# Gathers beside the first table: 28 dense expert columns for 48, and one pace for 58 gathered bursts

## The chip, the core and the metric

One NeuronCore of a Trainium2 chip runs the whole program in one launch. The engines are TensorE (PE; PEld is its weight load), VectorE (DVE), ScalarE (ACT), GpSimd (POOL) and SyncE (SP); 16 DMA engines move data between HBM and the on-chip memory SBUF. TensorE's sums lie in PSUM, eight banks of 128 partitions x 512 floats. The metric is the device time of one execution in microseconds (us), the median of several.

## The reference

A decoder layer on 256 tokens of width 2048: an RMSNorm with adaptive shift and scale, a token mixer (recurrent and state-space heads), and then PEER, a mixture of 128 x 128 = 16,384 one-neuron experts. The change lies in PEER alone, which is this:

```python
q = jnp.einsum("bsd,de->bse", h, w_q)...            # 8 heads, two halves of 128
sub_val, sub_idx = lax.top_k(sub, 16)               # 16 best of 128 keys per half
cand_idx = sub_idx[..., 0, :, None] * 128 + sub_idx[..., 1, None, :]
top_val, top_pos = lax.top_k(cand_val, 16)          # 16 of 256 pairs per head
gate = jax.nn.softmax(top_val, axis=-1)
act = jax.nn.gelu(jnp.einsum("td,thkd->thk", xt, u_tab[e]))
out = jnp.einsum("thk,thkd->td", g * act, v_tab[e])  # 128 experts a token
```

So each token has 128 (expert, gate) pairs. The expert number is 128 i + j. The kernel's inputs lay both tables out by the second key j: a "column" is the 128 experts with one j, 1 MB of U and 1 MB of V.

## The kernel before

All products are split into a high and a low part (`issue_split`: ScalarE copies the rounded half, VectorE subtracts), so a weight tile of 128 x 1024 floats ("tick", 0.5 MB) needs one ScalarE and one VectorE instruction. Tiles are loaded four ahead (NRAW) and split four ahead (NHL).

PEER treats columns in two ways. The first J1 = 80 columns (`u_quad`, 20 blocks of four columns, 160 ticks of 12 matmuls, lines 1467 to 1469): the product of every token with every expert goes to a DRAM array `ad`. For their second table, the (token, expert) pairs are sorted into lists: 32 tokens form a block g, 128 list places a row m; four blocks with the same m make a "quad". There are two lists (tokens 0 to 127, 128 to 255) of GL = 23 rows each, 46 quads. A quad's work: four indirect DMAs fetch one number each per place out of `ad` (`w_gather`, line 1519), four fetch 128 rows of V, 8 KB each (`v_gather`, line 1509), into one of seven row buffers; `w_make` applies the gelu and the gate and spreads the result over a 128 x 32 matrix per block; `v_quad` (line 1541) multiplies, 16 matmuls of 32 columns. Sums stay in PSUM banks 0 to 3 until a list is done.

The last JD = 48 columns are dense: `u_slot` (two ticks a column, lines 453 and 455) gives all tokens' products, times a dense table `Wt` of gates; `v_slot` (line 1637, two ticks a column, one for each half of the width) multiplies with V.

The order on every engine is written out by hand. Steps beside the main loop stand in a background queue `bg` that each tick pays for with 1.0 (`bg_pay`), a step costing 1.3 to 3.5; `defer` puts the elementwise half of a step behind the next tick. In `u_quad` these are the top-16 searches, the first list (`l_step`, `l_dec`), and 32 steps of the dense table (`g_step`: VectorE makes one-hot matrices, GpSimd multiplies in two halves of the gate, TensorE sums, ScalarE evacuates). The second list is made in the dense ticks, every fourth of which runs one list step (`tick`). From there a pace spreads the quads: quad q runs once q < 44 (n - 3) / 188 at dense tick n. The seven row buffers are filled before (`rows_first`). `gate2_tick` takes the last section of the adaLN product along on VectorE.

## Time and profile before

| | |
|---|---|
| time, median of 3 | 2092.22 us (2092.17 to 2098.64) |
| profiled execution | 2095.62 us, its span 2093.9 us |
| PE busy | 2017.4 us (96%) |
| DVE, ACT, POOL busy | 71%, 46%, 36% |
| DMA | 620.50 MB, 296 GB/s over the span |
| first table by blocks (`u_quad`) | 847 to 1337 us, DMA at 238 GB/s |
| dense columns, first table (`u_slot`) and quads | 1337 to 1703 us, DMA at 368 GB/s |
| dense columns, second table (`v_slot`) and quads | 1703 to 2065 us, DMA at 381 GB/s |

The page's rows of busy tenths cut the span into 40 slices; the windows view gives the busy time of each engine in chosen stretches; the DMA view gives packets, bytes and the share of the 16 engines' time by queue: q1 is SP's, q10 ScalarE's, q0 GpSimd's indirect DMAs.

### The profile page before, as it was taken

The numbers are of one execution on the slowest core, as the hardware profiler recorded it, in microseconds if no ns is written. First come the engines' busy times: TensorE is split into PE (matmuls) and PEld (weight loads), VectorE is DVE, ScalarE is ACT, GpSimd is POOL, SyncE is SP. The second block draws the span as 40 slices with busy tenths as digits, with TensorE's granted clock in tenths as the row PEclk, the third lists the DMA queues.
The fourth block names the chain that finished last, engine by engine and source line by source line (L and its number), as shares of the span: only waits on it lengthen the run. The fifth ranks groups of instructions, "written<-read, shape, count | busy, mean of one in ns | idle before, by whom it ended". The sixth has DMA issues, their size and how long they took to land. (4 is left out here: it accounts for less than half of the span.)

```text
span 2093.9 us, 34021 instructions
## 1 busy us (share of the span) xinstructions
PE 2017.4 (96%) x12742; PEld 1624.9 (78%) x12742; DVE 1489.5 (71%) x2211; ACT 963.7 (46%) x1457; POOL 745.6 (36%) x600
## 2 busy tenths in 40 slices
PE   7999999999999999999999999999999999998996
PEld 4789998989999898888787777776777766666663
DVE  3368897898878868879979999766555445454444
ACT  3446665677744454444443454433333333333332
POOL 0013344232212010000500477565556545554553
PEclk9999999999999999999999999999999999999999
DMA  9967767778789955668786677789999979999993
GB/s 387 406 233 250 230 225 230 230 241 295 273 295 344 332 177 181 197 224 278 228 272 214 204 258 247 251 336 407 387 400 394 407 280 404 420 411 362 417 412 113
DMA packets 237949, 620.50 MB, mean 296 GB/s; under 512 B 25352, under 2 KB 109496, under 8 KB 215480
## 3 DMA queue, kind: packets, MB, share of 16 engines
q1 hardware_dynamic: 188992, 387.76, 53.4%
q0 software_dynamic: 32384, 175.44, 20.9%
q10 hardware_dynamic: 16400, 55.06, 7.1%
q8 instruction: 102, 1.67, 0.3%
q14 instruction: 71, 0.58, 0.1%
HBM read 621.07 MB, written 14.72 MB: 304 GB/s over the span
## 5 line engine op out<-in xcount | busy, mean ns | idle before, releaser
L148 ACT ACTIVATE hl<-raw 128x1024 fp32r<-128x1024 f32 x594 | 628.8, 1061 | 1001.9 <-PE b L455 214.4
L157 DVE TENSOR_TENSOR hl<-raw,hl 128x1024 fp32r<-128x1024 f32 x594 | 765.0, 1295 | 114.6 <-ACT hl L148 102.5
L453 PE MATMUL b<-H,hl 128*128 128x512 f32 x1376 | 494.0, 402 | 1.4 <-ACT X L674 1.0
L455 PE MATMUL b<-H,hl 128*128 128x256 f32 x1376 | 385.7, 280 | 2.4 <-DVE hl L157 2.4
L453 PEld LDWEIGHTS b<-H,hl 128*128 128x128 f32 x1376 | 259.1, 188 | 81.0 <-issue 19.4
L1637 PE MATMUL b<-hl,X 128*128 128x512 f32 x1152 | 271.5, 394 | 11.5 <-DVEq L1753 6.4
L1637 PEld LDWEIGHTS b<-hl,X 128*128 128x128 f32 x1152 | 215.0, 189 | 77.5 <-issue 25.8
L455 PEld LDWEIGHTS b<-H,hl 128*128 128x128 f32 x1376 | 260.3, 189 | 4.0 <-DVE hl L157 3.1
L1467 PE MATMUL b<-hl,H 128*128 128x512 f32 x640 | 255.0, 398 | 0.0
L1469 PE MATMUL b<-hl,H 128*128 128x512 f32 x640 | 250.4, 391 | 2.2 <-DVE hl L157 2.2
L1468 PE MATMUL b<-hl,H 128*128 128x512 f32 x640 | 249.7, 390 | 0.0
L1519 POOL DMA_INDIRECT X<-ad,X x184 | 205.6, 1117 | 83.0 <-issue 55.7
L1541 PE MATMUL b<-tk,Wz 128*32 128x512 f32 x848 | 169.7, 602 | 7.5 <-DVE X L1531 4.6
L1509 POOL DMA_INDIRECT tk<-in_v_t,X x106 | 126.6, 1195 | 140.4 <-PE b L1541 116.1
L808 PE MATMUL b<-H,hl 128*128 128x256 f32 x560 | 162.9, 291 | 0.4 <-DVE ggt L465 0.4
L810 PE MATMUL b<-H,hl 128*128 128x256 f32 x560 | 159.5, 285 | 1.3 <-DVE hl L157 1.3
L809 PE MATMUL b<-H,hl 128*128 128x256 f32 x560 | 159.5, 285 | 0.0
L1541 PE MATMUL b<-vq,Wz 128*32 128x512 f32 x624 | 144.2, 598 | 0.4 <-DMA vq<-in_v_t,X 0.4
L1469 PEld LDWEIGHTS b<-hl,H 128*128 128x128 f32 x640 | 120.4, 188 | 28.8 <-DVE hl L157 3.0
L1468 PEld LDWEIGHTS b<-hl,H 128*128 128x128 f32 x640 | 120.8, 189 | 23.5
L393 DVE SCALAR_TENSOR_TENSOR adacc<-adr,cact,adacc 128x1024 f32<-128x1024 f32 x90 | 124.7, 1385 | 20.1 <-DMA adr<-in_w_ada 20.0
L1467 PEld LDWEIGHTS b<-hl,H 128*128 128x128 f32 x640 | 120.6, 188 | 23.0
(373 smaller groups left out, 3199.8 us busy)
## 6 DMA issues: line engine op xcount, KB each, us to landing
raw<-in_u_t SPq DMA_DIRECT2D x208, 512.0 KB
raw<-in_w_in SPq DMA_DIRECT2D x146, 512.0 KB
adr<-in_w_ada SPq DMA_DIRECT2D x96, 512.0 KB
adw<-in_w_ada SPq DMA_DIRECT2D x64, 512.0 KB
raw<-in_w_o SPq DMA_DIRECT2D x64, 512.0 KB
raw<-in_u_t ACTq DMA_DIRECT2D x48, 512.0 KB
raw<-in_v_t SPq DMA_DIRECT2D x48, 512.0 KB
raw<-in_v_t ACTq DMA_DIRECT2D x48, 512.0 KB
```

What stands on the lines that cost most here:

```text
L148: act.activation(t[:, 0], r, AF.Copy)
L157: dve.tensor_sub(t[:, 1], r, t[:, 0].bitcast(FT))
L453: pe.matmul(ps, w[:, 0, c], x[:, k].rearrange("p a b -> p (a b)"), start=(k == first), stop=False, skip_group_check=True)
L455: pe.matmul(ps[:, :256], w[:, 1, c], x[:, k, 0], start=False, stop=(k == 15), skip_group_check=True)
L808: pe.matmul(ps, wh, hT[:, k, 0, :], start=(k == 0), stop=False)
L809: pe.matmul(ps, wh, hT[:, k, 1, :], start=False, stop=False)
L1467: pe.matmul(o, hh, w[:, 0, :, kk], start=(k == 0), stop=False)
L1468: pe.matmul(o, hl_, w[:, 0, :, kk], start=False, stop=False)
L1469: pe.matmul(o, hh, w[:, 1, :, kk], start=False, stop=(k == 15))
L1519: pool.indirect_dma_start(wA[:, n % 32:n % 32 + 1], None, adf, bass.IndirectOffsetOnAxis(ap=LW[:, tb, g, m:m + 1], axis=0), bounds_check=T ...
L1541: pe.matmul(sb[c][32 * g:32 * g + 32, :], Wz[:, q % NW, g], vs[(4 * q + g) % NROW][:, c * 512:(c + 1) * 512], start=(m == 0), stop=(m == G ...
L1637: pe.matmul(ob[tb * 2 + c], w[:, i, s], v[:, k, c * 512:(c + 1) * 512], start=(jj == 0 and (i, k) == (0, 0)), stop=(jj == JD - 1 and k == 1))
```

## The change

JD falls to 28, so that 100 columns are gathered and `u_quad` has 25 blocks, 200 ticks. Each list gets two parts: places 0 to 13 (GA) hold experts with j < 48, places 14 to 28 (GB) those with 48 <= j < 100; GL is 29 and there are 58 quads. `ad` becomes two arrays, the first of which is complete after 12 of the 25 blocks. Both lists are now made inside `u_quad`, ahead of the dense table's steps. When the first list is done, `open_sparse` starts gathers, and from then on one counter of ticks, first-table and dense ticks alike, paces all quads. Their order is: list 0 first part, list 1, list 0 second part; the first part's sums are stashed in `S0` and added later. Row buffers: six from then on, eight once the first table is done. PSUM: first-table sums rotate through banks 0 to 2, lists and dense-table steps share bank 3, quads have banks 4 to 7. The dense table's gate multiply is one VectorE operation on both halves. The fallback `spill` follows the split of `ad`; it does not run with these inputs.

GpSimd, around the first gathers. `tk`, `vq`, `vx` are row buffers, `ohr`, `lists` and `two` hold lists and one-hot matrices, X_8024 and `lsm` the gathered numbers and list tables. Before (the dense table's multiplies, then the last rows and the first weight gathers, at the end of `u_quad`):

```order
L1372 TENSOR_TENSOR ohr<-ohr,lists 128x8x48
L1373 TENSOR_TENSOR ohr<-ohr,lists 128x8x48
L1694 MEMSET vq_12931 128x2048
L1509 DMA vq_12931<-in_v_t,X_8024 128x2048
L1694 MEMSET vq_12936 128x2048
L1509 DMA vq_12936<-in_v_t,X_8024 128x2048
L1519 DMA X_8024<-ad,X_8024 128x1 x9
L1509 DMA tk<-in_v_t,X_8024 128x2048
```

Now (at tick 112 of 200):

```order
L1539 MEMSET tk 128x2048 x4
L1539 MEMSET vq_10822 128x2048
L1539 MEMSET vx 128x2048
L1562 DMA lsm<-ad_8715,X_8024 128x1
L1549 DMA tk<-in_v_t,X_8024 128x2048
...
L1549 DMA vx<-in_v_t,X_8024 128x2048
L1562 DMA lsm<-ad_8715,X_8024 128x1 x12
```

The buffers are cleared together before the first gather, weight gathers stand between the row gathers, and the multiplies are gone from the engine.

TensorE, between two first-table ticks (a new place for a quad; before, only list and dense-table steps stood between first-table ticks):

```order
L1501 MATMUL b_12283<-hl,H 128x512
L1590 MATMUL b_11493<-vq_10822,Wz 32x512
L1590 MATMUL b_11493<-vx,Wz 32x512
L1590 MATMUL b_11493<-tk,Wz 32x512 x2
L1590 MATMUL b_11494<-vq_10822,Wz 32x512
...
L1590 MATMUL b_11496<-tk,Wz 32x512 x2
L1499 MATMUL b_12282<-hl,H 128x512
```

The quad's sums (b_11493 to b_11496, one bank each) stay open over such ticks; the next tick's matmuls stand behind the quad.

ScalarE, at the dense table's steps (`Wt`, its evacuation; `hl`, the split of a weight tile). Before, and then now:

```order
L148 ACTIVATE hl<-raw 128x1024
L1450 ACTIVATE Wt<-b_11320 128x8x24 x2
L148 ACTIVATE hl<-raw 128x1024
L1450 ACTIVATE Wt<-b_11363 128x8x24 x2
L148 ACTIVATE hl<-raw 128x1024 x2
```

```order
L149 ACTIVATE hl<-raw 128x1024
L1576 ACTIVATE lsm<-lsm 128x4
L149 ACTIVATE hl<-raw 128x1024
L1483 ACTIVATE Wt<-b_12261 128x8x14 x2
L149 ACTIVATE hl<-raw 128x1024
L1483 ACTIVATE Wt<-b_12308 128x8x14 x2
```

The order of split and evacuation is kept, a quad's gelu (`lsm`) stands between, and b_12261 and b_12308 are now the same bank where b_11320 and b_11363 were two.

The diff, cut to its core:

```diff
-JD = 48
+JD = 28
...
-GL = 23
+JA = 48
+GA, GB = 14, 15
+GL = GA + GB
...
 def p_ew2():
+            dve.tensor_tensor(pos, pa, V[0], op=OP.mult)
+            dve.scalar_tensor_tensor(x, pb, 128.0 * GA, V[1], op0=OP.add, op1=OP.mult)
+            dve.tensor_tensor(pu, pos, x, op=OP.add)
...
         if e == 15:
-            bg.extend(fin_steps())
-            bg.extend(l_step(0, n) for n in range(16))
-            bg.append((None, lambda: l_dec(0), 1.5))
+            f1, f2 = fin_steps()
+            bg.extend(f1)
+            bg.extend(l_step(0, n) for n in range(5))
+            bg.extend(f2)
+            bg.extend(l_step(0, n) for n in range(5, 16))
+            bg.append((None, lambda: (l_dec(0), open_sparse()), 2.0))
+            bg.extend(l_step(1, n) for n in range(16))
+            bg.append((None, lambda: (l_dec(1), sq.update(lists=False)), 2.0))
             bg.extend(g_step(n) for n in range(32))
...
 def prep():
-            dve.tensor_tensor(o[:, :, 1, :], bc(LS["iota16"][:, None, J1:], 128, NG, JD),
+            e = LS["eg"][:, n % 2]
+            dve.tensor_tensor(e, bc(LS["iota16"][:, None, J1:], 128, NG, JD),
                               bc(jT[:, s, None], 128, NG, JD), op=OP.is_equal)
-            pool.tensor_tensor(o[:, :, 0, :], o[:, :, 1, :], bc(LS["fld"][:, 2, s, None], 128, NG, JD), op=OP.mult)
-            pool.tensor_tensor(o[:, :, 1, :], o[:, :, 1, :], bc(LS["fld"][:, 3, s, None], 128, NG, JD), op=OP.mult)
+            dve.tensor_tensor(o, bc(e[:, :, None, :], 128, NG, 2, JD),
+                              bc(LS["fld"][:, 2:4, s].rearrange("p f t -> p t f")[:, :, :, None], 128, NG, 2, JD),
+                              op=OP.mult)
...
 def u_quad(n, pay):
-        ps = [bank(2 * (n % 2) + tb) for tb in range(2)]
+        ps = [bank((2 * n + tb) % 3) for tb in range(2)]
         for kp in range(8):
-            for kk in range(2):
-                k = 2 * kp + kk
-                for tb in range(2):
+            for kk, tb in ((0, 0), (1, 0), (0, 1), (1, 1)):
+                    k = 2 * kp + kk
...
+            if kp == 7:
+                t = keep.tile([128, 2, 512], FT, name="X2")
+                for tb in range(2):
+                    act.activation(t[:, tb], ps[tb], AF.Copy)
...
-            if it >= 22 and it % 2 == 0:
+            if it >= 22 and it % 2 == 0 or it >= 160:
                 gt["slot"] = it
                 gate2_tick()
+            tick()
...
+    quads = ([(0, m) for m in range(GA)] + [(1, m) for m in range(GL)] + [(0, m) for m in range(GA, GL)])
+    def v_feed(k=99):
+        while free and k and sq["g"] < 4 * NQD:
+            q, g = divmod(sq["g"], 4)
+            tb, m = quads[q]
+            if sq["lists"] and tb:
+                return
+            x = buf[sq["g"]] = free.pop(0)
+            pool.indirect_dma_start(x, None, vf, bass.IndirectOffsetOnAxis(ap=LV[:, tb, g, m:m + 1], axis=0),
+                                    bounds_check=E1 - 1, oob_is_err=False)
...
+    def w_feed(k=99):
+        while k and sq["w"] < 4 * min(NQD, sq["n"] + 4):
...
+            i = int(m >= GA)
+            if i and not sq["stored"] or sq["lists"] and tb:
+                return
...
     def sparse():
+        sq["n"] += 1
+        w_feed(1)
+        v_quad(q)
+        for g in range(4):
+            w_feed(1)
+            v_feed(1)
+    def first_rows():
+        for x in range(4):
+            add_row(tk[:, x * D:(x + 1) * D])
+        add_row(s1.tile([128, D], FT, name="vq4", tag="ts1"))
+        add_row(vx)
+    def open_sparse():
+        gbk[:] = [3]
+        sq.update(on=True, first=False, all=8 * NU - sq["at"] - 1 + 4 * JD)
+        for _ in range(6):
+            w_feed(1)
+            v_feed(1)
     def tick():
...
-        if n >= 6 and sq["n"] < (NQD - 2) * (n - 3) // (4 * JD - 4):
+        w_feed()
+        w_make()
+        v_feed()
+        q = sq["n"]
+        if (q < (NQD - 2) * (n - 3) // (sq["all"] - 3) and sq["made"] > q
+                and sq["g"] >= 4 * q + 4 and not (q == GA + GL - 1 and sq.get("rows", n) > n - 8)):
             sparse()
...
-    tick()
     mid()
     mid()
-    final(0)
-    sparse()
     final(1)
+    sparse()
+    final(0)
```

More of the change, by code (lines that the diff above doesn't have):

```diff
@@ L1070, in hybrid_kernel @@
     for tb in range(2):
-        a = s1.tile([128, 1808], FT, name=f"ts{tb}")
+        a = s1.tile([128, 2128 if tb == 0 else 1800], FT, name=f"ts{tb}")
         TK.append(dict(v16=a[:, 0:256].rearrange("p (e k) -> p e k", e=16),
@@ L1318, in gate2_tick @@
         n = gt["n"]
-        if n >= 64:
+        q, k = divmod(n, 16)
+        if n >= 64 or sq["first"] or (k == 0 and gt["fin"] < q - 1):
             return
-        q, k = divmod(n, 16)
         if n == 0:
@@ L1399, in l_ew @@
                 prep()
-                if n == 15:
+            elif n == 15:
+                for _ in range(3):
                     prep()
@@ L1534, in v_quad @@
     def v_quad(q):
-        tb, m = divmod(q, GL)
-        if m == 0:
+        tb, m = quads[q]
+        a, b = (0, GA) if tb == 0 and m < GA else (GA, GL) if tb == 0 else (0, GL)
+        if m == a:
             for c in range(4):
-                sb[c] = bank(c)
+                sb[c] = bank(4 + c)
         for c in range(4):
             for g in range(4):
-                pe.matmul(sb[c][32 * g:32 * g + 32, :], Wz[:, q % NW, g], vs[(4 * q + g) % NROW][:, c * 512:(c + 1) * 512],
-                          start=(m == 0), stop=(m == GL - 1), skip_group_check=True)
@@ L1543, in v_quad @@
-        if m == GL - 1:
-            for c in range(4):
-                merge(tb, c, sb[c])
-    sq = {"n": 0, "it": 0, "w": 0}
-    late = []
+                pe.matmul(sb[c][32 * g:32 * g + 32, :], Wz[:, q % NW, g], buf[4 * q + g][:, c * 512:(c + 1) * 512],
+                          start=(m == a), stop=(m == b - 1), skip_group_check=True)
+        free.extend(buf.pop(4 * q + g) for g in range(4))
+        if m == b - 1:
+            if b == GA:
+                for c in range(4):
+                    act.activation(S0[:, c * 512:(c + 1) * 512], sb[c], AF.Copy)
+            else:
+                for c in range(4):
+                    merge(tb, c, sb[c])
@@ L1553, in sparse @@
     def sparse():
         q = sq["n"]
-        if q < NQD:
-            sq["n"] += 1
-            w_gather()
-            v_quad(q)
-            for g in range(4):
-                if g:
-                    w_gather()
-                v_gather(4 * q + NROW + g)
-            late.append(lambda: w_make(q + 1))
+        if q >= NQD:
+            return
+        while sq["made"] <= q:
+            sq["it"] += 3
+            w_feed()
[3 more added lines that the diff above has]
+        v_quad(q)
@@ L1565, in tick @@
+        for g in range(4):
+            w_feed(1)
[11 more added lines that the diff above has]
+            v_feed(1)
     def tick():
+        if not sq["on"]:
+            return
@@ L1567, in tick @@
         sq["it"] += 1
-        n = sq["it"]
-        while late:
-            late.pop(0)()
-        if n == 2:
-            for _ in range(8):
-                w_gather()
-        if n == 5:
-            w_make(0)
-        if n <= 2 * JD and n % 4 == 0:
-            if n == 4:
-                prep()
-                prep()
-            if n <= 64:
-                f, e = l_step(1, n // 4 - 1)[:2]
-                f()
-                defer(e)
-            if n == 68:
-                l_dec(1)
@@ L1703, in hybrid_kernel @@
             bg_flush()
-            assert gt["n"] == 64 and not pedue and len(gpend) == 0
+            assert gt["n"] == 64 and not pedue and len(gpend) == 0 and sq["on"]
             g2p = gbank()[:16, :128]
@@ L1724, in spill @@
         for tb in range(2):
-            b = [bank(4 + c) for c in range(4)]
+            b = [bank(c) for c in range(4)]
             for t in range(128):
```

243 lines of the change are left out of this document (131 added, 112 removed).

## Prediction

> **What bounds the kernel now.** I read the page first, then the stretches, then the queues. A "tick" below is one half-megabyte weight tile and the twelve (or sixteen) matmuls on it; a "quad" is four gathered blocks of up to 128 rows and their matmuls.
>
> ```profile
> PE 2017.4 (96%) x12742; PEld 1624.9 (78%) x12742; DVE 1489.5 (71%) x2211; ACT 963.7 (46%) x1457; POOL 745.6 (36%) x600
> ...
> DMA  9967767778789955668786677789999979999993
> ```
>
> TensorE looks like the bound everywhere. The DMA row says otherwise for the last third: 9 from slice 27 on, but 6 to 8 in the first-table stretch ahead of it. The stretches, from the windows view (columns: PE, PEld, DVE, ACT, POOL busy, clock, DMA share, GB/s); the last two rows are the same windows for line 1469 alone, of which four belong to a tick:
>
> ```profile
> 847.00:1084.00 237.00, 234.85 (x1061) 194.38 (x1059) 199.36 (x394) 104.63 (x122) 33.95 (x18) 1.00 0.75 242
> 1084.00:1177.00 93.00, 87.39 (x490) 69.81 (x489) 89.38 (x115) 32.93 (x35) 8.99 (x4) 0.98 0.66 217
> 1177.00:1337.00 160.00, 151.16 (x1090) 120.79 (x1089) 156.45 (x142) 81.05 (x125) 111.31 (x74) 1.00 0.75 246
> ...
> 1386.00:1680.00 294.00, 293.60 (x1933) 212.23 (x1932) 158.45 (x257) 106.42 (x174) 173.28 (x147) 1.00 1.00 399
> 1720.00:2050.00 330.00, 321.20 (x1720) 215.25 (x1719) 159.20 (x252) 122.63 (x198) 178.66 (x163) 0.99 0.99 399
> ...
> 847.00:1084.00 237.00, 131.00 (x336) 63.06 (x336) 1.00 0.75 242
> 1084.00:1177.00 93.00, 44.08 (x112) 21.32 (x112) 0.98 0.66 217
> ```
>
> So ticks 0 to 83 of the first table run at TensorE's pace, ticks 84 to 159 at VectorE's (89.38 of 93 us, 156.45 of 160 us: the lists and the dense one-hot tables), and from 1386 us on TensorE and the DMA engines are full together. There a gain on TensorE alone is worth nothing. What the change asks is whether bytes moved into the half-used stretch cost less than the work that leaves.
>
> **The change on TensorE.** Pitches, from the timeline (first table, then dense first-table columns) and the chain of waits (dense second-table ticks, a quad):
>
> ```profile
> 899.93 0.39 PE L1469 MATMUL b<-hl,H 128*128 128x512 f32 x1
> 902.65 0.39 PE L1469 MATMUL b<-hl,H 128*128 128x512 f32 x1
> ...
> 1499.71 0.39 PE L453 MATMUL b<-H,hl 128*128 128x512 f32 x1
> 1504.66 0.40 PE L453 MATMUL b<-H,hl 128*128 128x512 f32 x1
> ...
> 1956.05 11.10 PE b L1637 x48
> 1967.15 3.57 PE b L1541 x32
> ...
> L1440 PE MATMUL b<-ohr,two 128*128 128x48 f16 x512 | 20.2, 184 | 8.6 <-POOL ohr L1373 8.5
> L1637 PE MATMUL b<-hl,X 128*128 128x512 f32 x1152 | 271.5, 394 | 11.5 <-DVEq L1753 6.4 <-ACT X L446 4.9
> ```
>
> Between the first two rows lie 12 matmuls: 0.2267 us each, 2.72 us a tick. Between the next two lie 14 pairs of a 512- and a 256-wide matmul: 0.3536 us a pair, 5.66 us a column. Forty-eight matmuls in 11.10 us are 2.775 us a tick, 5.55 us a column; a quad (32 records) is 3.57 us. A dense-table step is 20.2/32 = 0.63 us; I take that for a list step too.
>
> Removed: 20 dense columns x (5.66 + 5.55) = 224 us. Added: 5 blocks of four columns x 8 ticks x 2.72 = 109 us, and 12 quads (46 to 58) x 3.57 = 43 us. TensorE's own sum falls by 72 us. This would be the gain if nothing else bound.
>
> **Where the quads go.** The lists of the first 128 tokens close at tick 112 of 200, and the pace is 56 quads over the 200 ticks left (88 first-table, 112 dense): one each 3.5 ticks. By the built order 25 quads stand beside first-table ticks, the first behind tick 117, and 33 beside or behind the dense ones. Call these stretches S1 and S2. That the gathers do begin early is thus settled; only their price is open.
>
> **Start of S1.** Before, tick 112 begins at 1177 us. Up to there the change takes 14 gate steps and 3 dense-table steps off VectorE and adds wider list steps (116 columns, not 92) and some ten small operations; I take 1174 us.
>
> **DMA in S1 and S2.** From the queue view of three windows (850 to 1080, 1400 to 1680, 1720 to 2050 us), and of 5 us around two early gathers beside first-table loads (1232 and 1209 us); columns are packets, MB, share of 16 engines:
>
> ```profile
> q1 hardware_dynamic: 50107, 55.70, 74.7%
> ...
> q0 software_dynamic: 12221, 72.22, 64.0%
> q1 hardware_dynamic: 5408, 19.72, 17.7%
> ...
> q0 software_dynamic: 14424, 84.21, 62.2%
> ...
> q0 software_dynamic: 144, 1.05, 64.5%
> ...
> q0 software_dynamic: 144, 1.05, 58.9%
> ```
>
> First-table loads (1 KB packets, one queue): 55.70 MB in 0.747 x 230 us = 324 GB/s at a full share. Gathers (8 KB rows) among dense loads: 72.22 MB in 0.640 x 280 us = 403, and 84.21 in 0.622 x 330 = 410 GB/s. A lone gather beside first-table loads: 1.05 MB in 0.645 x 5 us = 325, and in 0.589 x 5 us = 356 GB/s. A dense tile of 0.524 MB: 19.72 MB in 0.177 x 280 us = 398 GB/s, 1.3 us. Dense stretch in all: 399 GB/s.
>
> The Trainium skill ("DMA: Bandwidth & Descriptors", Specifications) puts full line rate from 512 bytes up; first-table loads would then run like gathers, and S1 below would be 36 us shorter. This trace disagrees, 324 against 403 to 410 GB/s. The same page (Where 436 GB/s comes from) has HBM to SBUF bound at about 358 GB/s a core; the 335 MB below would then take 936 us and the kernel end near 2139 us. The trace shows 399 GB/s for 294 us, so I give that rule no chance here.
>
> By the reference's own routing 26,288 of the 32,768 (token, expert) pairs fall in the first 100 columns (21,400 in the first 80, which is the page's 175 MB); a full quad is 512 rows, 4.19 MB, and quads 13, 27, 41, 42, 56 and 57 are all but empty.
>
> S1: 81 tiles still to load (42.5 MB; about 7 of the 88 are ahead already), 32 gate tiles (8.4) and 11.5 stores (6.0) are 57 MB: 176 us at 324 GB/s. Quads 0 to 24 and the six rows ahead are 12,900 rows, 105.7 MB. The trace has no back-to-back gathers beside 1 KB loads; the ends are 410 (258 us) and 325 GB/s (325 us). What slows the lone gathers is likelier their lone start than the 1 KB neighbours, so I take 391, a quarter of the way down: 270 us. S1 = 446 us (434 to 501).
>
> TensorE in S1: 88 x 2.72 + 25 x 3.57 + 32 x 0.63 + 16 x 0.63 = 358 us, 90 us below: the DMA engines set S1.
>
> S2: 58.7 MB of dense tiles, 4.2 MB of rows and constants, 13,388 rows (109.7 MB). A period of 3.6 ticks with a full quad carries 6.09 MB, at 408 GB/s 14.9 us; TensorE needs 3.6 x 2.8 + 3.57 = 13.7 us. 27 such periods and 4 near-empty ones at 13.7 are 457 us; tiles loaded ahead (up to 8 ticks of 1.3 us) hide about 10 us at each of two near-empty places: 437. Two quads behind the last tick (7 us) and the two changes of phase (8 us, of the 11.5 that line 1637 idles now): S2 = 452 us (439 by TensorE alone, 472 without the hiding).
>
> **Other engines.** The dense table's two multiplies leave GpSimd and become one VectorE operation; table 1's list steps move into S1.
>
> ```profile
> L157 DVE TENSOR_TENSOR hl<-raw,hl 128x1024 fp32r<-128x1024 f32 x161 | 217.8, 1367 | 17.3 <-ACT hl L148 17.2
> L1370 DVE TENSOR_TENSOR ohr<-lists,ohr 128x384 f16<-128x384 f16 x32 | 23.2, 725 | 0.0
> L1377 DVE TENSOR_TENSOR two<-lists 128x1024 fp8e4<-128x1024 f16 x16 | 19.5, 1220 | 0.0
> L1381 DVE TENSOR_TENSOR lists<-lists 128x736 f16<-128x736 f16 x16 | 14.8, 926 | 1.9 <-DVE lists L1379 0.5
> ...
> L1330 DVE SCALAR_TENSOR_TENSOR adgx<-two,cact,adgx 128x512 f32<-128x512 f32 x30 | 28.3, 943 | 12.4 <-DMA two<-in_w_ada 12.3
> ...
> L1532 DVE TENSOR_TENSOR Wz<-Wz,X 128x128 f32<-128x128 f32 x44 | 12.9, 293 | 1.5
> L1529 DVE TENSOR_TENSOR Wz<-X,LC 128x128 f32<-128x128 f32 x44 | 12.6, 285 | 0.0
> L1531 DVE SCALAR_TENSOR_TENSOR X<-X,LG 128x4 f32<-128x4 f32 x44 | 7.7, 175 | 132.2 <-ACT X L1528 39.1 <-DMA X<-ad,X 35.4 <-ACT hl L148 28.8
> ...
> L1372 POOL TENSOR_TENSOR ohr<-ohr,lists 128x384 f16<-128x384 f16 x32 | 50.3, 1571 | 128.5 <-DVE ohr L1370 127.4 <-PE b L1469 0.5 <-DVE mod L1339 0.5
> ...
> L148 ACT ACTIVATE hl<-raw 128x1024 fp32r<-128x1024 f32 x160 | 170.1, 1063 | 268.0 <-PE b L1469 163.1 <-DMA raw<-in_u_t 71.1 <-DVE hl L157 8.3
> L1450 ACT ACTIVATE Wt<-b 128x192 f32<-128x192 f32 x64 | 27.3, 533 | 0.7 <-DVE hl L157 0.7
> L1486 ACT ACTIVATE X<-b 128x512 f32<-128x512 f32 x38 | 20.5, 590 | 0.0
> ...
> L1519 POOL DMA_INDIRECT X<-ad,X x184 | 205.6, 1117 | 83.0 <-issue 55.7
> L1509 POOL DMA_INDIRECT tk<-in_v_t,X x106 | 126.6, 1195 | 140.4 <-PE b L1541 116.1
> ```
>
> VectorE in S1: 88 x 1.37 + 32 dense steps x about 2.2 (1.22 + 0.42 + 0.56, by elements) + 16 list steps x 2.8 + 32 gate steps x 0.94 + 25 quads x 0.75 = about 285 us of 446: hidden, and still under TensorE's 358 if that cover went. GpSimd loses 64 x 1.57 = 100 us and issues 4 x 1.12 + 4 x 1.20 = 9.3 us a quad, under either period. Six row buffers are a quad and a half: the last two blocks of the next quad wait on GpSimd for the quad that frees them, weight gathers queued behind; two pairs of issues (4.6 us) and two blocks (2.1 MB at 391 GB/s, 5.4) make 10 us, while 3.5 ticks take TensorE at least 9.5: even, so it adds nothing while DMA sets the pace. ScalarE: the dense steps now share one PSUM bank, and in 16 places two steps stand a tick apart; the second waits on TensorE, a quad or the next tick behind it, for a split (1.06) and two evacuations (2 x 0.45), 2.0 us, 32 us in all, under the 88 us that TensorE waits in S1 anyhow. First-table sums rotate through three banks: a block's second half of tokens needs a bank whose evacuation (0.59) has six matmuls (1.36 us) as cover: nothing.
>
> **Sum.** The last merges and the output take now:
>
> ```profile
> 2078.73 1.06 PE b L1541 x5
> ...
> 2087.81 0.66 DVEq L1832
> ```
>
> From TensorE's end (2079.8) to the span's end, 14 us, kept. 1174 + 446 + 452 + 14 = 2086 us of span, against 2093.9. The profiled run's time was 2095.6, 3.4 above the median of the three; span less 1.7 is the median's scale: **2084 us**, 0.4% less. A measurement here tells 0.3% (6 us) from no change.
>
> **Rivals.** (1) *The bytes hide.* TensorE sets both stretches: 1174 + 358 + 32 + 439 + 14 - 2 = 2015 us. For it: DMA is at 0.75 before the dense part. Against: 335 MB would have to pass in about 820 us, 409 GB/s throughout, 1 KB loads among them. It could go part of the way, 2015 to 2055. (2) *Mixing costs* (slower side). All gathers of S1 run as the two lone ones: 105.7 MB at 333 GB/s are 317 us, S1 = 493, the end 2131. Tiles on the one queue then come late, the splits with them, and TensorE waits at each tick. It decides (slower than 2098) once gathers in S1 fall under 372 GB/s. For it: the two rows are the only ones with this mix. Against: they are single gathers after a pause. (3) *The shared bank.* If the engines idle while a dense step waits, its 32 us add: 2116. Against: loads run up to 8 ticks ahead, longer than 2 us.
>
> **Chances.** Forecast 0.48 (its own range 2060 to 2106), (1) 0.17, (2) 0.27, (3) 0.08. The forecast splits 0.26 faster, 0.17 same, 0.05 slower; with (1) faster, (2) 0.25 slower, (3) mostly slower: faster 0.43, same 0.21, slower 0.36. Range: 2040 leaves out most of (1), 2125 the worse half of (2).
>
> **What would show it.** Right: in S1 a DMA share of 0.97 or more at 365 to 390 GB/s, ticks of about 5.1 us with their quads, TensorE waiting for gathers at the quads' line; in S2 a share near 1.0, and a stretch of about 450 us. Wrong: a share below 0.9 in S1 (then some engine or the row buffers bind); S1 under 400 us; S1 over 480 us with gathers' share per MB as in the lone ones; TensorE's waits in S1 lying with the evacuations.

## The result: 1.1% slower, and where the time went

The changed kernel takes 2117.86 us (median of 4, 2114.3 to 2123.47), the kernel before 2095.23 (median of 4, 2092.17 to 2098.64): a ratio of 1.011, 95% interval 1.0079 to 1.0141. The forecast was 2084 and "faster"; 2118 lies inside its range (2040 to 2125), but on the other side of the kernel before. The profiled execution took 2114.3 us with a span of 2112.6, 18.7 more than the span before.

The page of the changed kernel, its share of busy time and the tenths of TensorE, the clock and the DMA engines in 40 slices of 53 us:

```profile
PE 1982.3 (94%) x12488; PEld 1552.0 (73%) x12488; DVE 1416.3 (67%) x2177; ACT 895.7 (42%) x1364; POOL 764.6 (36%) x637
...
PE   7999999999999999999989779888899999999897
...
PEclk9999999999999999999999899999999999999899
DMA  9967667777899855677665799999899899989994
```

TensorE's busy time fell by 35 us, and the span grew all the same. The DMA row is filled four slices earlier than before (8 and 9 from slice 23 on, counted from 0). In slices 22 to 28 TensorE, which stood at 9 almost throughout, falls to 7 and 8 (slice 24 excepted), and in slice 22 its clock falls too. The windows view cuts this at the end of S1 (tick 199, 1623 us) and of S2's first half (columns as in the prediction: PE, PEld, DVE, ACT, POOL busy, clock, DMA share, GB/s), then the two large queues in S1 and, as the last line, the gathers' queue from there to 2096 us (packets, MB, share of 16 engines):

```profile
1177.00:1623.00 446.00, 383.78 (x2492) 252.73 (x2493) 249.26 (x356) 123.30 (x204) 248.15 (x211) 0.95 0.95 359
1623.00:1850.00 227.00, 223.41 (x1408) 153.28 (x1407) 97.11 (x161) 79.19 (x133) 152.80 (x130) 0.99 0.99 401
1850.00:2101.00 251.00, 233.20 (x1248) 145.87 (x1248) 118.50 (x195) 79.95 (x136) 144.10 (x126) 0.97 0.87 349
...
q0 software_dynamic: 17609, 98.67, 55.6%
q1 hardware_dynamic: 51739, 59.50, 38.3%
...
q0 software_dynamic: 23079, 116.84, 60.4%
```

S1 is 446 us, the very number of the forecast, but not for its reason. The gathers pass at 98.67 MB / (0.556 x 446 us) = 398 GB/s, where 391 was assumed, SyncE's queue at 348, not 324: 248 + 171 = 419 us of DMA time where 446 had been reckoned. Most of this difference is bytes, not speed: the sum put 105.7 MB of gathers into S1 and 109.7 into S2, and measured are 98.67 and 116.84. Seven MB (18 us at 391 GB/s) pass later than reckoned; the better rates are worth 9 us. So 27 us of S1 are time that the transfers of these two queues did not need. Only 24 quads start before the end of tick 199; the 25th, which the sum had in S1, starts 5.6 us behind it. TensorE's own sum in the S1 measured here is therefore 355 us, not 358; below, 358 and S2's 433 stand as the prediction counts the quads.

A balance over all that follows tick 112, up to the last quad (the tail behind it is 11.5 us before and 11.4 now). By the pitches of the prediction TensorE's own sum was 48 x 2.72 + 48 x 0.63 + 48 x 11.21 + 46 x 3.57 = 863 us and is now 88 x 2.72 + 48 x 0.63 + 28 x 11.21 + 58 x 3.57 = 791: 72 us less, as forecast. The stretch itself went from 905 to 924 us. So the time over TensorE's sum grew from 42 to 133 us. Before, ticks 112 to 159 took 160 us for a sum of 151, and the rest 745 for 712; now S1 takes 445 for 358 and S2 479 for 433. Most of the growth, about 80 us, lies in S1. The experiments divide these 133.

The trace alone divides S1's part. TensorE is idle for 62 us of S1: 33 at the shared bank, where the dense-table and gate steps wait for ScalarE (the 24.9 in the list below is most of it), 22 for VectorE's work on list 2, and only 4 for gathered rows. Its matmuls take 383 us, some 25 more than their sum. In the clock's records the granted clock stands at one half for 48 us of S1, during 34 of which matmuls run; that accounts for about 17 of the 25.

What the waits view of S1 offers as suspects (us in total, times, longest):

```profile
DVE lsm L1579 <- ACT lsm L1576: 88.8, 18, 11.9
...
DVE ohr L1356 <- DMA two<-in_w_ada: 27.9, 6, 7.0
...
PE b L1474 <- ACT Wt L1483: 24.9, 13, 3.9
PE b L1426 <- DVE lists L1415: 22.4, 5, 10.0
DVE adgx L1356 <- DMA two<-in_w_ada: 22.0, 8, 6.8
```

The longest of these, VectorE behind ScalarE's gelu, no run removed. It is 106.3 us in gates_out and 127.3 in early_q_pack below, whose S1 are 14 and 48 us shorter, so its size does not follow S1's length.

And one place in full, from the timeline behind the opening of the gathers (start, length, engine, line; in brackets the idle time ahead and what ended it):

```profile
1193.76 1.28 ACT L1576 ACT_TABLE_LOAD   x1 [11.95 <-DMA lsm<-ad,X]
...
1195.29 0.17 DVE L1579 SCALAR_TENSOR_TENSOR lsm<-lsm,LG 128x4 f32<-128x4 f32 x1 [11.91 <-ACT lsm L1576]
...
1199.64 0.93 PE L1426 MATMUL b<-lists,two 128*128 128x116 f16 x8 [10.03 <-DVE lists L1415]
1200.34 0.77 PE L1499 MATMUL b<-hl,H 128*128 128x512 f32 x1
1200.91 0.63 PE L1500 MATMUL b<-hl,H 128*128 128x512 f32 x1
```

Read downwards, it is one late transfer handed on: the numbers for the first quad come behind gathered rows, so ScalarE stands 12 us ahead of its gelu; VectorE stands behind the gelu, though the next step of list 2 lies ready behind it; TensorE stands 10 us for that list; and then its matmuls take 0.63 us where they take 0.39. The granted clock is 0.50 from 1191.8 to 1205.4 us, that is, from inside the wait until 5.8 us after it, and the clock of S1 is 0.95 in the mean. The Trainium skill ("TensorE: Matmul & The Clock Gate", Part 1) says that an idle TensorE falls to half rate and comes back only after some 3.4 us of work. The trace agrees on the half rate; here the way back took 5.8 us.

### The profile page after: what moved, and what is told of

Same layout as the page of the kernel before. It is cut to its first block, busy times and chain, and to the rows that moved or that the text cites. A ratio compares the mean times of both kernels' runs of the same rounds, so it can differ in the third digit from the quotient of the medians.

```text
span 2112.6 us, 33462 instructions
## 1 busy us (share of the span) xinstructions
PE 1982.3 (94%) x12488; PEld 1552.0 (73%) x12488; DVE 1416.3 (67%) x2177; ACT 895.7 (42%) x1364; POOL 764.6 (36%) x637
## 5 line engine op out<-in xcount | busy, mean ns | idle before, releaser
L149 ACT ACTIVATE hl<-raw 128x1024 fp32r<-128x1024 f32 x554 | 585.1, 1059 | 1038.7 <-PE b L1501 295.1
L158 DVE TENSOR_TENSOR hl<-raw,hl 128x1024 fp32r<-128x1024 f32 x554 | 699.8, 1270 | 134.7 <-ACT hl L149 133.7
L454 PE MATMUL b<-H,hl 128*128 128x512 f32 x1056 | 377.6, 401 | 1.1 <-ACT X L675 1.1
L1499 PE MATMUL b<-hl,H 128*128 128x512 f32 x800 | 326.5, 408 | 0.5 <-ACT X L1505 0.5
L1501 PE MATMUL b<-hl,H 128*128 128x512 f32 x800 | 317.9, 397 | 2.1 <-DVE hl L158 2.1
L1500 PE MATMUL b<-hl,H 128*128 128x512 f32 x800 | 317.6, 397 | 0.0
L1562 POOL DMA_INDIRECT lsm<-ad,X x232 | 267.0, 1151 | 131.0 <-issue 68.8
L456 PE MATMUL b<-H,hl 128*128 128x256 f32 x1056 | 295.6, 280 | 2.4 <-DVE hl L158 2.4
L454 PEld LDWEIGHTS b<-H,hl 128*128 128x128 f32 x1056 | 198.2, 188 | 61.4 <-issue 12.1
L456 PEld LDWEIGHTS b<-H,hl 128*128 128x128 f32 x1056 | 199.2, 189 | 4.0 <-DVE hl L158 3.0
L1499 PEld LDWEIGHTS b<-hl,H 128*128 128x128 f32 x800 | 153.8, 192 | 50.5 <-issue 20.1
L1501 PEld LDWEIGHTS b<-hl,H 128*128 128x128 f32 x800 | 153.6, 192 | 37.6 <-DVE hl L158 3.6
L1500 PEld LDWEIGHTS b<-hl,H 128*128 128x128 f32 x800 | 154.0, 192 | 29.9
L1690 PE MATMUL b<-hl,X 128*128 128x512 f32 x672 | 162.4, 401 | 9.4 <-DVEq L1806 5.7
L1690 PEld LDWEIGHTS b<-hl,X 128*128 128x128 f32 x672 | 128.0, 193 | 50.3 <-issue 18.3
L809 PE MATMUL b<-H,hl 128*128 128x256 f32 x560 | 161.7, 289 | 0.4 <-DVE ggt L466 0.4
L811 PE MATMUL b<-H,hl 128*128 128x256 f32 x560 | 158.4, 283 | 1.3 <-DVE hl L158 1.3
L810 PE MATMUL b<-H,hl 128*128 128x256 f32 x560 | 158.4, 283 | 0.0
```

Source lines behind the costliest of these rows:

```text
L149: act.activation(t[:, 0], r, AF.Copy)
L158: dve.tensor_sub(t[:, 1], r, t[:, 0].bitcast(FT))
L454: pe.matmul(ps, w[:, 0, c], x[:, k].rearrange("p a b -> p (a b)"), start=(k == first), stop=False, skip_group_check=True)
L456: pe.matmul(ps[:, :256], w[:, 1, c], x[:, k, 0], start=False, stop=(k == 15), skip_group_check=True)
L809: pe.matmul(ps, wh, hT[:, k, 0, :], start=(k == 0), stop=False)
L810: pe.matmul(ps, wh, hT[:, k, 1, :], start=False, stop=False)
```

## The experiments

Two theories stood at the start. Theory D: from tick 112 on the DMA engines set the time, and the engines' waits are idle time that the transfers would have taken anyhow. Theory W: waits handed on in program order, as in that timeline, set it, and the DMA engines are only nearly full.

All times are medians, beside the kernel before on the same chip; S1 (tick 112 to the end of tick 199) and S2 (from there to the end of the last quad) come from the profiled execution. Two versions that leave S1 as it is (no_rows, fng_early) have it at 451.4 and 451.7 us, so one S1 is good to about 6 us. The kernel before itself has medians from 2093.3 to 2098.3 us beside the various runs; differences of a few us between two versions are read from the ratios and their intervals.

| run | us | ratio to before (95%) | tick 112 at | S1 | S2 |
|---|---|---|---|---|---|
| before | 2095.2 | 1 | 1177.2 | (160) | (745) |
| the change | 2117.9 | 1.011 (1.0079 to 1.0141) | 1177.4 | 445.3 | 478.5 |
| half_rows | 2055.9 | 0.9825 (0.9801 to 0.985) | 1179.6 | 416.0 | 445.1 |
| pack4k | 2112.9 | 1.0087 (1.0067 to 1.0107) | 1176.8 | 446.7 | 481.4 |
| gate_actq | 2118.1 | 1.0111 (1.0088 to 1.0133) | 1179.7 | 446.7 | 480.3 |
| dense_apart | 2103.9 | 1.0046 (1.0029 to 1.0063) | 1177.3 | 434.1 | 484.4 |
| weights_first | 2126.3 | 1.0152 (1.0113 to 1.0192) | 1180.0 | 449.6 | 478.5 |
| gate_early | 2150.8 | 1.0263 (1.0213 to 1.0312) | 1237.3 | 419.3 | 481.4 |
| three | 2129.7 | 1.0146 (1.0103 to 1.0189) | 1237.5 | 405.2 | 482.4 |
| before_half | 2085.1 | 0.9949 (0.9931 to 0.9968) | 1172.8 | (160) | (738) |
| half_quads | 2265.9 | 1.0786 (1.0761 to 1.0811) | 1180.3 | 504.8 | 567.1 |
| early_q | 2092.5 | 0.9957 (0.9937 to 0.9977) | 1195.8 | 410.1 | 477.7 |
| half_apart | 2046.1 | 0.9733 (0.9695 to 0.9772) | 1181.1 | 394.9 | 459.2 |
| hq_early_q | 2237.5 | 1.0655 (1.0632 to 1.0677) | 1191.3 | 457.5 | 567.4 |
| early_q_pack | 2083.8 | 0.9954 (0.9939 to 0.9969) | 1196.3 | 397.8 | 477.4 |
| gates_out | 2098.7 | 1.0014 (1.0 to 1.0028) | 1177.5 | 431.0 | 477.7 |
| no_rows | 2121.9 | 1.0126 (1.0111 to 1.0142) | 1185.0 | 451.4 | 483.4 |
| late_quads | 2240.8 | 1.0692 (1.0673 to 1.0712) | 1175.6 | 342.4 | 707.1 |
| fng_early | 2116.2 | 1.0086 (1.0055 to 1.0117) | 1177.6 | 451.7 | 476.7 |
| best | 2087.8 | 0.9958 (0.9941 to 0.9975) | 1195.2 | 396.0 | 478.3 |

**Bytes or waits: half of each row.**

```diff
+    vh = v_t.rearrange("j i (h d) -> (j i h) d", h=2)
...
-            pool.indirect_dma_start(x, None, vf, ...
+            pool.indirect_dma_start(x[:, :D // 2], None, vh, ...
```

> The changed kernel, with each gathered row cut to 4 KB (1024 of its 2048 numbers, taken from half rows of the table): half of the bytes of every gather is left out, 108 of 642 MB; every instruction, list, wait and matmul stays. Theory D (the DMA engines set the time from tick 112 on): some 52 MB fall out of S1 and 55 MB out of S2, at about 395 GB/s 130 and 140 us, until TensorE's own sums (358 us and 439 us) and what it waits for engines stop the gain: S1 375 to 400 us, S2 about 440 us, the time 2010 to 2040 us. Theory W (waits of the engines for one another, in program order, set it; DMA is only nearly full): 2095 to 2118 us, S1 still above 430 us.

```profile
1180.00:1596.00 416.00, 375.57 (x2484) 249.29 (x2483) 247.58 (x355) 123.40 (x204) 254.54 (x212) 0.96 0.81 267
1596.00:2041.00 445.00, 439.27 (x2655) 294.27 (x2653) 215.92 (x356) 159.23 (x270) 285.72 (x255) 0.99 0.78 268
```

Both theories missed: 62 us, not the 78 to 108 of the one and not the 0 to 23 of the other. S2 is the clean half. With half of the gathered bytes TensorE is busy 439 of 445 us; with all of them S2 takes 33 us more. So the gathered bytes make S2 longer than TensorE alone would; whether by the DMA engines' rate (their share is 1.02 from 1722 to 1850 us, but 0.87 in the second half) or by rows that come late into few row buffers, this run does not tell. S1 loses only 29 us of 445 although 49 MB are gone and the DMA share is 0.81. Something else holds it 58 us above TensorE's sum of 358: TensorE is idle for 40 us of it, of which rows account for 1.

**Packet size.**

```diff
-            items.append(u_t[4 * n:4 * n + 4, :, kp * 256:(kp + 1) * 256].rearrange("j p c -> p j c"))
+            items.append(u_q[n, kp])     # u_q: [J1 / 4, 8, 128, 1024], laid out so on the host
```

> The changed kernel with the first table's blocks laid out in HBM as they are used, so that a tile is 128 pieces of 4 KB where it was 512 pieces of 1 KB; same bytes, same instructions. Theory D: the 48 MB of first-table tiles in S1 pass at about 400 GB/s, not at the 324 I reckoned: 28 us less, 2088 to 2092 us, all of it in S1; ahead of tick 112 nothing, since VectorE and TensorE set the pace there. Theory W: within 6 us of 2118. If packet size is not what makes those loads dear: the same 2118.

5 us by the medians, with overlapping intervals, and S1 unchanged. SyncE's queue (first-table and gate tiles, in S1 stores too) in two windows, 850 to 1080 us and 1177 to 1595, first of the change, then with 4 KB pieces:

```profile
q1 hardware_dynamic: 49560, 55.42, 73.4%
...
q1 hardware_dynamic: 51042, 57.40, 39.6%
```

```profile
q1 hardware_dynamic: 18936, 56.14, 72.8%
...
q1 hardware_dynamic: 19429, 57.18, 36.6%
```

In the first window, beside no gathers, the loads run at 328 and 335 GB/s of full share: pieces four times as long change next to nothing, so the 324 GB/s that I had blamed on 1 KB packets are not theirs. In S1, beside gathers, 347 becomes 374 GB/s, 13 us of DMA time; but S1 was not waiting for that alone.

**The gate tiles' place in the queue.**

```diff
-            sp.dma_start(gt[n], w_ada[...])
+            (act if sq["on"] else sp).dma_start(gt[n], w_ada[...])
```

> The changed kernel with the gate tiles of S1 (0.25 MB each, for the last adaLN section) issued on ScalarE's DMA queue, so that they no longer queue behind the weight tiles on SyncE's; same bytes, same arithmetic. Theory W: VectorE loses its 27.9 + 22.0 us of waits for these tiles in S1, the splits behind them come earlier, and the time falls by 15 to 30 us, to 2088 to 2103. Theory D: within 6 us of 2118; a byte moved from one queue to another is still a byte.

No change. VectorE's waits for the tiles in S1 fell from 49.9 us to 12.9, TensorE's for list 2 from 22.4 us to 12.5, and S1 took as long: idle time taken away in one place came back in another.

```profile
PE b L1426 <- DVE lists L1415: 12.5, 3, 9.9
```

**The shared bank.**

```diff
 def g_step(n):
-        return g_pe, g_ew, 1.5
+        return g_pe, g_ew, 2.0
```

> The changed kernel with the dense table's 32 steps paid for with 2.0, not 1.5, so that two of them never stand one tick apart, and a step's evacuation out of the shared bank has a whole tick and more before the next step; nothing else differs. Theory W: TensorE's 24.9 us of waits for these evacuations in S1 go, and the time falls by 15 to 25 us. Theory D: within 6 us of 2118, the wait being idle time that a later wait for the weights would have taken.

14 us less: just under what theory W gave it, and against theory D. TensorE's waits for the evacuation fall from 24.9 us to 6.4, and S1 by 11. A new wait of TensorE, 15.1 us for a gate step on VectorE, takes part of their place, and S2 is 6 us longer. This is the prediction's third rival, at less than half its price (32 us).

```profile
PE b L1474 <- ACT Wt L1483: 6.4, 2, 6.1
```

**The opening's order.**

```diff
-        for _ in range(6):
-            w_feed(1)
-            v_feed(1)
+        w_feed(6)
+        v_feed(6)
```

> The changed kernel with the opening's twelve first indirect DMAs in another order: six fetches of the gathered numbers first, then the six rows, where they alternated; nothing else differs. In the trace of the change ScalarE stands 11.95 us before the first gelu, whose numbers come behind rows of 1 MB, and the splits, VectorE's lists and TensorE stand behind it. Theory W (waits handed on in program order): ticks 112 to 127 take 8 to 12 us less and the time is 2104 to 2111 us. Theory D (bytes): those ticks are made good later, 2114 to 2121 us.

No gain: 8 us slower by the medians, with overlapping intervals. ScalarE's wait ahead of the first gelu falls from 11.95 us to 5.3. But the first row is issued some 8 us later, the first quad starts at 1214.9 us, not 1207.2, and ticks 112 to 119 take 6.19 us each instead of 5.33. Ticks 120 to 127 make that good, so that the sixteen take 90.5 us for 94.2, short of the 8 to 12 that theory W gave them, and the end is no earlier. The chain in the timeline above is real; that it costs time at the end is not shown.

**The gate steps ahead of S1.**

```diff
-            if it >= 22 and it % 2 == 0 or it >= 160:
+            if it >= 22:
```

> The changed kernel with a step of the last adaLN section on every first-table tick from tick 22 on, not on every second one: all 64 are over before tick 112, so 8.4 MB and 32 VectorE steps (30 us) leave S1 for the stretch ahead of it, where the DMA share is 0.75. Since the gate tiles' waits alone were worth nothing (their own queue: no change), theory W now expects only what list 2 gains on VectorE, 0 to 8 us. Theory D: 8.4 MB at 400 to 415 GB/s, 20 us, 2095 to 2102 us. Either could lose up to 10 us ahead of tick 112 where VectorE is full (ticks 84 to 111).

Tick 112 came 60 us later, far beyond the 10 allowed for; from there on 24 us were gained. The waits from 848 to 1237 us say why it was late:

```profile
DVE adgx L1356 <- DMA two<-in_w_ada: 29.9, 17, 3.6
PEld b L1501 <- DVE hl L158: 28.2, 27, 3.2
DVE ohr L1356 <- DMA two<-in_w_ada: 23.7, 12, 4.6
PE b L1501 <- DVE hl L158: 17.5, 13, 2.7
```

With one tick instead of two between a tile's issue and its use, VectorE stands 53.6 us for tiles behind the weights on SyncE's queue (in the change 23.5 up to tick 112), and TensorE's matmuls 17.5 and its weight loads 28.2 for the subtractions behind them (the two can overlap). Up to tick 112 TensorE is idle for 44 us, where it is idle for 11 in the change, and its matmuls take 345 us for 323, at a mean clock of 0.95 for 0.99.

**The three edits together** (dense_apart, weights_first, gate_early):

> The changed kernel with the three edits together: fetches of numbers before rows at the opening, the gate steps over before it, and the dense table's steps a tick and more apart. If S1 is a row of waits handed on, with the DMA engines idle in between, the three add up: 14 us measured for the steps, 8 to 12 for the opening, 0 to 20 for the gate tiles: 2072 to 2096 us, under the kernel before. If the DMA engines' bytes are the next bound at once, the sum stops near S1 = 405 us (152 MB at 375 GB/s): 2078 us at the least. If they overlap: 2096 to 2104 us.

From tick 112 on 37 us less, the 60 ahead of it not made good.

**A control: the kernel before with half rows** (the edit of half_rows, in its `v_gather`):

> A control: the kernel before, its gathered rows cut to 4 KB in the same way (88 of 620 MB left out, the sums of the right half of the width not being the reference's). It tells what bound its dense stretch, of which I had read that TensorE and the DMA engines are full together. Theory D (bytes set it): TensorE's own sum from 1337 us on is 48 columns of 11.2 us, 46 quads of 3.57 and some list steps, 712 us of the 743 measured, so 2060 to 2070 us. If TensorE set it: 2085 to 2094 us.

```profile
1333.00:2071.00 738.00, 721.87 (x4289) 501.56 (x4287) 382.24 (x616) 271.30 (x445) 405.44 (x362) 0.99 0.76 257
```

10 us, of which 7 lie in the dense stretch (the others lie ahead of tick 112, where nothing differs). TensorE set that stretch, although the DMA share in it stood at 1.00: a full share says that the engines had something under way, not that anything waited for them.

**Quads in halves.**

```diff
...
-        sq["n"] += 1
+        gs = (2, 3) if sq["h"] else (0, 1)
+        sq["n"] += sq["h"]
+        sq["h"] = 1 - sq["h"]
         w_feed(1)
-        v_quad(q)
-        for g in range(4):
+        v_quad(q, gs)
+        for g in range(2):
...
```

> The changed kernel with each quad run as two halves of two blocks, about 1.75 ticks apart, so that row buffers come free two at a time and TensorE is held 1.8 us, not 3.57, by a burst; same matmuls, gathers and bytes. Theory R (the burst and the six row buffers, a quad and a half, make TensorE and the DMA engines wait in turns): S1 and S2 both lose part of what they have over the larger of TensorE's and the bytes' time, 15 to 40 us together: 2078 to 2103 us. If that coupling is not it: 2112 to 2124 us.

148 us slower, and it does not answer its question. Half a quad costs TensorE as much as a whole one. The timeline, first of the change, then of halves:

```profile
1703.19 0.62 PE L1590 MATMUL b<-vx,Wz 128*32 128x512 f32 x1
1703.20 1.03 PE L1590 MATMUL b<-vq,Wz 128*32 128x512 f32 x3
1703.65 0.59 PE L1590 MATMUL b<-vx,Wz 128*32 128x512 f32 x1
1703.65 1.01 PE L1590 MATMUL b<-vq,Wz 128*32 128x512 f32 x3
```

```profile
1703.79 0.62 PE L1590 MATMUL b<-vq,Wz 128*32 128x512 f32 x1
1703.79 0.62 PE L1590 MATMUL b<-vx,Wz 128*32 128x512 f32 x1
1704.24 0.59 PE L1590 MATMUL b<-vq,Wz 128*32 128x512 f32 x1
1704.24 0.59 PE L1590 MATMUL b<-vx,Wz 128*32 128x512 f32 x1
```

Four 32-column products run side by side, a new set every 0.43 to 0.46 us; with two of them the pitch is the same. So TensorE's sum grew by 58 x 3.57 = 207 us: S1 should be 358 + 89 = 447 and is 505, again 58 more; S2 should be 433 + 118 = 551 and is 567, now 16 more where bytes had made it 46.

**Gate steps early, on another queue, with dense steps apart.**

```diff
-            sp.dma_start(gt[n], w_ada[...])
+            act.dma_start(gt[n], w_ada[...])
...
-            if it >= 22 and it % 2 == 0 or it >= 160:
+            if it >= 22:
...
-        return g_pe, g_ew, 1.5
+        return g_pe, g_ew, 2.0
```

> The changed kernel with the gate steps on every tick (over before tick 112), their tiles on ScalarE's DMA queue, and the dense table's steps a tick and more apart. With the tiles on SyncE's queue the early steps put tick 112 off by 60 us, 53 us of it VectorE waits for tiles that had one tick, not two, to come past the weight tiles; from there on 24 us were gained. If that queueing was the loss, tick 112 now starts at 1180 to 1195 us and the end is 2080 to 2098 us. If the 32 extra steps of 0.94 us on VectorE were the loss, tick 112 stays at 1215 us or later and the time is 2110 to 2130 us.

As the first case had it: tick 112 at 1195.8, S1 410.1, and 2092.5 us, 1.2% under the change and 0.4% under the kernel before (interval 0.2 to 0.6%). The queueing was two thirds of gate_early's 60 us; 18 us remain, which may be the steps' own, though no run shows it.

**Half rows and dense steps apart** (both edits above):

> The changed kernel with the gathered rows cut to 4 KB (half of the gathered bytes left out, as in the earlier run, 2056 us) and the dense table's steps a tick and more apart. The first of these runs left S1 at 417 us with the DMA engines at 0.8: a floor made by engines. If the shared bank's waits (21.8 + 5.3 us of TensorE there) make that floor, S1 falls to 390 to 400 us and the time to 2030 to 2040 us. If they are hidden under another wait: 2050 to 2058 us.

S1 falls to 394.9, but S2 rises by 14; from tick 112 to the last quad it is 854 us for 861, and the median falls by 10. Between the two expectations: part of the bank's 27 us is path, part is hidden; why S2 rises is open.

**Everything with quads in halves** (half_quads and early_q):

> All that may help, as a candidate: quads in halves, gate steps early with tiles on ScalarE's queue, dense steps apart. If the three gains add (15 to 40, 20, 14 us): 2044 to 2070 us, under the kernel before by 1 to 2%. If the bytes after tick 112 (330 MB at 400 to 415 GB/s, 795 to 825 us) and the tail (16 us) end it: 1185 + 810 + 16 = about 2010 us at the least. If quads in halves are worth nothing: as early_q.

As early_q, plus the halves' price (145 us). S1, 457.5 us, is now 10 over TensorE's sum of 447, where half_quads was 58 over.

**4 KB pieces once the waits are gone** (early_q and pack4k):

> The version that beat both (gate steps over before tick 112 with their tiles on ScalarE's queue, dense steps a tick and more apart; 2092 us) with the first table's tiles in pieces of 4 KB. Alone the 4 KB pieces brought 5 us, in a stretch that waits of engines held open. If, those gone, S1 (now 410 us, DMA share 0.97 to 1.03) is bound by the DMA engines, the pieces count: 60 MB at 374 and not 347 GB/s, 13 us, and 2075 to 2082 us. If S1 is still held by engines: 2086 to 2094 us.

2083.8 us, 8.6 less than early_q by the medians; but beside the kernel before the two are alike (0.9954 and 0.9957), so the time does not decide between the two cases. In the profiled executions S1 is 12 us shorter, by the same edit that brought S1 nothing beside the waits.

```profile
1196.00:1594.00 398.00, 373.19 (x2474) 241.32 (x2474) 228.96 (x325) 122.47 (x203) 256.96 (x210) 0.97 0.97 383
1594.00:2071.00 477.00, 457.50 (x2658) 299.66 (x2656) 216.64 (x356) 159.90 (x271) 296.47 (x256) 0.98 0.93 374
```

S1 is now 40 us over TensorE's sum and its DMA engines carry 383 GB/s, not 359.

**Gate tiles left out.**

```diff
-            sp.dma_start(gt[n], w_ada[...])
+            sq["on"] or sp.dma_start(gt[n], w_ada[...])
```

> The changed kernel without the loads of the 32 gate tiles of S1 (8.4 MB left out; the 32 VectorE steps and their sums still run, on old tiles, so the last adaLN section is wrong). Moving steps and tiles ahead of S1 took 24 us out of S1 and later; moving the tiles to another queue nothing. If it was their bytes: 17 to 25 us less, 2093 to 2101 us. If it was the steps on VectorE: within 6 us of 2118.

19 us, and S1 14 shorter in the profile: the bytes, not VectorE's steps, which all still run. VectorE's waits for the tiles are gone too, but gate_actq took 37 of their 49.9 us away and gained nothing; on the other queue the bytes had cost the same.

**Row loads left out.**

```diff
-            sp.dma_start(R["t"][:, 3], ...)      # and three more
+            dve.memset(R["t"][:, 3], 1.0)
```

> The changed kernel without the four loads of rows in the second half of S2 (gate, residual and norm rows, 4.2 MB; the constants 1.0 stand in their place, so the sums are not the reference's). S2 takes 33 us over TensorE's sum, most of it in its second half (246 us for 212). If that is plain bytes, 4.2 MB give back 10 us. If it is the place of these loads on SyncE's queue (in the trace it stands 21.5 us before the last of them, for the gathers ahead, with weight tiles behind it), 20 to 30 us: 2088 to 2098.

No gain (its profiled execution took 2133.0 us, 11 over the median). The wait that SyncE had at the last of these loads, first fence, stands on VectorE instead, second fence:

```profile
SPq L1713 <- DMA vq<-in_v_t,X: 21.5, 1, 21.5
```

```profile
DVE H L1713 <- DMA vq<-in_v_t,X: 22.0, 1, 22.0
```

**The gathers' early start undone.**

```diff
-        if (q < (NQD - 2) * (n - 3) // (sq["all"] - 3) and sq["made"] > q
+        if (q < (NQD - 2) * (n - 3 - (sq["all"] - 4 * JD)) // (4 * JD - 3) and sq["made"] > q
```

> The changed kernel with one part undone: the pace of the quads begins with the dense columns (six rows are still fetched early), so that all 58 stand in S2. S1 then has only its own work, 88 ticks at 3.3 to 3.5 us, about 300 us. S2 must pass 59 MB of tiles, 4 of rows and 211 of gathers, 274 MB at 399 GB/s, 687 us. 1177 + 300 + 687 + 17 - 2 = 2179 us. If S2 is held by TensorE instead (5.6 x 56 + 58 x 3.57 = 521 us), 2013 us.

```profile
1176.00:1518.00 342.00, 290.18 (x1714) 230.60 (x1713) 233.45 (x285) 119.38 (x176) 31.72 (x28) 0.93 0.60 202
1518.00:2225.00 707.00, 618.76 (x3425) 331.23 (x3423) 229.47 (x425) 163.80 (x296) 469.50 (x438) 0.97 0.94 381
```

With 28 dense columns the early start is worth 123 us (two executions). And S1 without a single quad takes 342 us, not 300. No engine is full in it: TensorE's own sum is 88 x 2.72 + 48 x 0.63 = 270, VectorE 233, DMA share 0.60. The 72 us over TensorE's sum need no quad, and no gathers beyond the six rows of the opening; they are there with the opening, the lists, the gate steps and the dense steps. TensorE is idle for 51 of the 72, mostly in these waits:

```profile
PE b L1474 <- ACT Wt L1483: 26.9, 16, 2.1
PE b L1426 <- DVE lists L1415: 17.7, 6, 10.0
```

The other 20 are the clock, at one half for 48 us of this S1, 41 of them with matmuls running.

**The last row load ahead of the fallback's branch.**

```diff
-                rows_load(3)
             v_slot(h, jj)
-            if h == 0 and jj in (0, 4, 12):
+            if h == 0 and jj in (0, 4, 12, 16):     # and rows_load(3) again inside the fallback
```

> The changed kernel with the last of the four row loads (the norm row, 1 MB) issued at dense tick 17 of S2's second half, ahead of the branch to the fallback, and again inside the fallback; bytes unchanged. Where it stood, SyncE was held 21.5 us for the gathers ahead (a place that the fallback would gather into), ScalarE 10 us for the weight tiles behind it; without the load the same wait moved to the instruction in its place. If that order is a part of S2's 33 us: 8 to 20 us less, 2098 to 2110 us. If S2 is bound by its bytes: within 6 us of 2118.

SyncE's wait of 21.5 us is gone from the trace, ScalarE's of 10.0 behind it is 1.5, and S2 is as long as it was. Idle time, not path.

**All four edits that were left** (early_q_pack and fng_early):

> The four edits that are left: gate steps over before tick 112 with their tiles on ScalarE's queue, dense steps a tick and more apart, first-table tiles in pieces of 4 KB, the norm row ahead of the branch. The first three together measured 2083.8 us. If the norm row's gain adds: 2068 to 2078 us. If S2 is bound by bytes: 2080 to 2087.

No better than without the last one. early_q, early_q_pack and best lie at 0.9954 to 0.9958 of the kernel before, not to be told apart by time. The lowest median is early_q_pack's: 0.5% under the kernel before, 1.6% under the change (2083.8 for 2117.9).

## Why the prediction was wrong, step by step

- **TensorE's own sum** (72 us less): right. The balance has it, and half_rows' S2 of 445 us lies within 6 us of the 439 that the prediction gave TensorE there.
- **Start of S1** at 1174: 1177.4.
- **S1 at 446, set by the DMA engines**: the number was right by luck, the step wrong. The step that failed is the one that let the DMA engines alone set S1 and gave the engines' waits nothing: VectorE "hidden", and the shared bank's 32 us "under the 88 us that TensorE waits in S1 anyhow". TensorE's 88 spare us were not slack under DMA: half of the gathers' bytes out left S1 58 us over TensorE's sum, no quad at all left it 72 over. The transfers needed 419 us, not 446, because 7 MB of gathers fell out of S1 (18 us) and the rates were better (9); the waits, put at nothing, filled these 27 us again. Of S1's 87 us over 358, 29 go with half of the gathered bytes, 58 stay. The shared bank has 11 to 14 of the 87, and leaving out the gate tiles' bytes, which the sum did count but at no place of their own, takes 14 out of S1 (19 out of the time); these shares overlap. Part of the 87, about 17, is the clock at one half behind the waits, which the prediction left out.
- **S2 at 452**: here the 27 us were lost. S2 is 478.5. The mis-sized term is the gathered bytes: 116.84 MB, not 109.7, 17 us at the sum's own 408 GB/s, the same 7 MB that S1 did not take. Some 9 us remain; the term "tiles loaded ahead hide about 10 us at each of two near-empty places" (20 us) may have them, but no run tests it alone. Every version with whole rows and whole quads lies within 6 us of 478.5, but for the one with all quads in S2. Half the rows' bytes give 33 us back; row loads and SyncE's order (no_rows, fng_early) nothing.
- **The sum.** Against 2086 the span is 26.6 more: start 3.4, S1 -0.7, S2 26.5, tail -2.6 (the last quad before ends at 2082.4 us, not at 2079.8, so the tail was 11.5 and not 14). Another 7 us lie in the step from span to median: 1.7 was taken off, and the change's median is 5.3 above its profiled span.
- **The rivals.** (1) fell. (2) was to decide under 372 GB/s of the gathers in S1; they ran at 398 and the end was on its side, by another way. (3) is partly true, at 14 us for 32: TensorE does wait 33 us at the shared bank, but taking most of that away gained less than half.
- **What was to show it.** Of the marks for "right", ticks of 5.1 us in S1 came true and the others did not (in S1 0.95 for 0.97, 359 GB/s for 365 to 390, 4 us of TensorE's waits at the quads' line; in S2 0.93 for near 1.0, 478 us for 450); of the marks for "wrong" only the last was met, in part (24.9 of TensorE's 62 idle us lay with the evacuations). A mark on TensorE's idle time by cause would have told more than one on the DMA share.

In early_q_pack S1 is still 40 us over 358: TensorE is idle for 25 of them (13 for list 2, 11.5 for gathered rows) and its matmuls take 15 longer. What removes these is open. Whether more row buffers would help was not settled, since halved quads changed TensorE's work; nor is it shown what limits S2's second half, or why 4 KB pieces run faster beside gathers but hardly alone.

## What to carry to other kernels

Work and bytes moved into a stretch where the DMA engines are half used bring what the waits of that stretch leave of the gain; first ask what the stretch takes with none of the new work in it (here 342 us, where the sum of any one engine said at most 270), and add to that. A share of 1.00 on the DMA engines does not mean that they bind, nor 0.95 that they do not: take bytes out and see. And a wait in the list is path only if its removal moves the end: of those tried here, the gate tiles' queue, SyncE's 21.5 us and the 12 us at the opening moved nothing forward. A wait of TensorE also costs more than its length, as its matmuls behind it run slower: without any quad, S1 had 51 us of waits and lost 20 more to the clock.
